# Projecting q and k of a head pair together, 512 moving columns at a time

## The chip, the cores and the metric

The kernel runs on one core of a Trainium2 chip. The metric is the device time of one execution in microseconds (us). The kernel before took 879.91, 881.80 and 883.73 us in three runs, median 881.8 us. Beside these, one execution was profiled; every duration below comes from it.

## The reference

One layer of a hybrid decoder on 512 tokens of width 1024, in float32:

```
h = rmsnorm(x)
[q | k | v | x_rnn | g_rnn | gate_attn | gate_rnn] = h @ W_in
A = differential attention (q and k normed per head half of 64, T5 bias, causal, 8 heads)
R = gelu(g_rnn) * RG-LRU(conv4(x_rnn))
x = x + (sigmoid(gate_attn) * (A @ P_attn) + sigmoid(gate_rnn) * (R @ P_rnn)) @ W_out
x = x + relu(rmsnorm(x) @ W_up)^2 @ W_down
```

q, k and v are 1024 wide each. A head has 128 columns of q and of k (two halves of 64, each with its own softmax; the second is subtracted with a learnt weight) and 128 of v.

## The kernel before, in words

**Numbers as pairs.** Every operand of a large matmul is a pair `hi`, `lo` in a rounded 32-bit format: ACT writes `hi` (a cast), DVE writes `lo` (source minus `hi`). A product is three matmuls, hi·hi, hi·lo, lo·hi (`mm3`, L124 to L127). The normed input is held as `hT`, transposed, in eight pieces of 128 features (k = 0 to 7).

**Weights.** `Weights` (L81) is a queue of units of 128 x 1024 numbers. SP fetches a unit into one of two raw buffers (`fetch`), ACT and DVE split it into a `whi`, `wlo` pair (`cast`). There are four pairs (`slots`); `get` takes the next unit, `free` gives its pair back, `pump` casts one more if a pair is free and fewer than `ahead` units are waiting.

**Stages.** An opening stage loads x, norms it and projects three gate blocks; then come attention, the recurrent branch, the merge and the MLP. The change lies in the end of the opening and in attention.

**A head pair.** `qkv_pair(j)` (L432) projects q, k and v of heads 2j and 2j+1. For each of the three, two units hold 4 k each of 256 weight columns. For each of four token tiles (128 tokens) `tok_proj` (L220) holds the tokens' piece of hT still in the array and moves the 256 weight columns past it: 8 k times 3 products, 24 matmuls with 256 moving columns. Two token tiles share a PSUM bank (`acc`, three banks). When a bank of q or k is full, `normed_a` squares it on ACT, sums the squares on DVE and takes the power -0.5 on POOL (`rs`); `normed_b` multiplies bank by `rs` into `qn` on DVE; `turn` transposes it on PE and splits it into `qkT`. A bank of v is split at once.

**The steps of attention.** 32 steps, four query tiles for each of eight heads. `logits(s)`: 6 small PE matmuls. `soft_a(s)`: DVE adds the bias and takes the maximum (two passes and `nm`), ACT takes the exponentials. `soft_b(s)`: four DVE operations that normalise and subtract. `turn(s)`: PE transposes the result, ACT and DVE split it into `pt`. `av`: PE multiplies by v. Step s issues logits(s), soft_a(s), soft_b(s-1) and turn(s-2):

```
order = [post_d, post_c, post_b, av, post_a, turn, logits, soft_a, soft_b]
```

Between steps `fill_in` runs pieces of the next pair's projection, by a budget of 3.6 a step; a token tile counts 2.6. Pair 0 is projected before the first step, pairs 1 to 3 during the 24 steps of pairs 0 to 2.

**What sets the order.** ACT, DVE and POOL keep the order in which the program issues (`InOrder`, L58), and each works strictly down its list in the profile. PE's list is set when the program is built: a scheduler takes, by its own estimate of times, what is ready first. On the chip PE works down that fixed list.

**Bias.** `toep`, eight resident tiles of 128 x 512, one per head, are loaded by SP from a table laid out in DRAM, in the first pair and the first steps.

Of the kernel before, what the change touches and what calls it, by code (L numbers as in the profile page):

```python
# [23 lines left out]
KT = DM // P  # L24
NH = 8
# [4 lines left out]
TW = 640  # L30
# [4 lines left out]


@with_exitstack
def tile_block(ctx: ExitStack, tc: tile.TileContext, x, w_in, w_rga, w_rgx, w_pa, w_pr, w_o,
               w_up, w_dn, rel_bias, smalls, lamv, onehot, out):
    nc = tc.nc  # L40

# [34 lines left out]
    def psum(tag):  # L76
        return pp.tile([P, 512], F32, tag=tag, name=tag, bufs=nb[tag])

    slots = [4]

    class Weights:  # L81
        def __init__(self, ahead, raws):
            self.reqs, self.raw, self.units = [], [], []
# [14 lines left out]
        def cast(self, pool=None):  # L98
            assert pool or slots[0] > 0
            slots[0] -= 0 if pool else 1  # L100
            self.fetch()
            n = len(self.units)
            raw, a = self.raw[n], self.reqs[n][1]
            hi, lo = ((pool or wp).tile([P, a, 1024 // a], F32R, tag=t, name=t, bufs=2 if pool else 4) for t in ("whi", "wlo"))
# [14 lines left out]
            return self.units[self.pos - 1]  # L119

        def free(self):
            slots[0] += 1

    def mm3(o, l, r, first, last):  # L124
        T.matmul(o, l[0], r[0], start=first, stop=False)  # L125
        T.matmul(o, l[0], r[1], start=False, stop=False)  # L126
        T.matmul(o, l[1], r[0], start=False, stop=last)  # L127
# [88 lines left out]
    def h_tok(k, t):  # L216
        ts = slice(t * P, (t + 1) * P)
        return hT[0][:, k, ts], hT[1][:, k, ts]

    def tok_proj(bank, ws, t):  # L220
        b = bank[:, 256 * (t % 2):256 * (t % 2) + 256]
        for k in range(KT):
            w = ws[k // 4]
            mm3(b, h_tok(k, t), (w[0][:, k % 4, :], w[1][:, k % 4, :]), k == 0, k == KT - 1)
            if t == NT - 1 and k % 4 == 3:
                wa.free()
        wa.pump()

    OQ, OK_, OV, OX, OG, OGA, OGR = (j * DM for j in range(7))
# [136 lines left out]
    def bias_table():  # L366
        parts = ((0, 512), (512, 128))
        ohs = []
        for c0, n in parts:
            o = work("oh")  # L370
            nc.sync.dma_start(o[:64, :n], onehot[:, c0:c0 + n])
            ohs.append(o)
        rb = sm.tile([64, 32], F32, name="rbt", tag="rbt", bufs=1)
        G.memset(rb, 0.0)
        G.memset(rb[32:33, :], MASKED)
        nc.sync.dma_start(rb[0:NBUCKET, 0:NH], rel_bias)
        yield
        for (c0, n), o in zip(parts, ohs):
            ps = psum("at")
            T.matmul(ps[:32, :n], rb, o[:64, :n], start=True, stop=True)  # L380
            tb = work("tb")
            V.tensor_copy(tb[:32, :n], ps[:32, :n])
            nc.sync.dma_start(tdram[:, c0:c0 + n], tb[:NH, :n])
        yield
        for h in range(NH):
            nc.sync.dma_start(trep[h].rearrange("o (r y) -> o r y", r=P),
                              tdram[h:h + 1, :].rearrange("h (o y) -> h o y", o=1).broadcast_to([1, P, TW]))
            yield
            t0 = trep[h][0:1, :]
            nc.sync.dma_start(toep[h], bass.AP(tensor=t0.tensor, offset=t0.offset + 127, ap=[[TW - 1, P], [1, S]]))  # L390

    def lam_diff(lt):
        lv = lt[:, :256].rearrange("p (a b c) -> p a b c", a=2, b=2)
# [36 lines left out]
        yield  # L430

    def qkv_pair(j, qk, v):  # L432
        def proj(o, bank):
            ws = [wa.get(), wa.get()]
            for t in range(NT):
                if t % 2 == 0:
                    bank.append(psum("acc"))
                tok_proj(bank[t // 2], ws, t)
                yield 2.6

        def normed_a(b, qn):
            n = wk.tile([P, S], F32, tag="qn", name="qn", bufs=4)
            A.activation(n, b, AF.Square)
            ss = sm.tile([P, 8], F32, tag="ss8", name="ss8")
            V.tensor_reduce(out=ss, in_=n.rearrange("p (g d) -> p g d", g=8), axis=AX.X, op=ALU.add)
            rs = sm.tile([P, 8], F32, tag="rs8", name="rs8")
            rstd_of(rs, ss, 64, 8)
            qn.append(n)
            return b, n, rs

        def normed_b(b, n, rs):
            V.tensor_tensor(out=n.rearrange("p (g d) -> p g d", g=8), in0=b.rearrange("p (g d) -> p g d", g=8),
                            in1=rs.rearrange("p (g o) -> p g o", o=1).broadcast_to([P, 8, 64]), op=ALU.mult)

        def turn(qi, qn, gsc, hh):
            ps = psum("at")
            for t in range(NT):
                c0 = 256 * (t % 2) + P * hh
                T.transpose(out=ps[:, t * P:(t + 1) * P], in_=qn[t // 2][:, c0:c0 + P], identity=ident)  # L459
            d = unit("qkT")  # L460
            split(d[:, 0, :], d[:, 1, :], ps, gsc)
            qk[hh, qi] = d

        banks = {o: [] for o in (OQ, OK_, OV)}
        qn = {o: [] for o in (OQ, OK_)}
        pend, half = [], []
        for o, qi, gsc in ((OQ, 0, qg), (OK_, 1, kg), (OV, None, None)):
            for t, cost in enumerate(proj(o, banks[o])):
                half.append(None)
                ready = half.pop(0) if len(half) > 2 else None  # L470
                if ready:
                    normed_b(*ready)
                if t % 2 == 1:
                    b = banks[o][t // 2]
                    if o != OV:
                        half[-1] = normed_a(b, qn[o])
                    else:
                        vt = wk.tile([P, 2, 2, 256], F32R, tag="v", name="v", bufs=4)
                        split(vt[:, 0], vt[:, 1], b.rearrange("p (t c) -> p t c", t=2))
                        v.append(vt)  # L480
                if pend and t >= 2:
                    turn(*pend.pop(0))
                    cost += 0.45
                yield cost
                if j == 0 and o == OV and t == 0:
                    lam_diff(lt)
                if j == 0 and o != OQ:
                    next(bt)
            if o != OV:
                pend = [(qi, qn[o], gsc, 0), (qi, qn[o], gsc, 1)]  # L490

    def attention(fills, qks, vs, pads):
        st = {}
# [97 lines left out]
        def at(step, f, *a):  # L591
            acts.setdefault(step, []).append((f, a))

        for s in range(NH * NT):
# [7 lines left out]
            if i == 3:  # L602
# [1 line left out]
                at(s + 4, post_b, h)  # L604
                at(s + 5, post_c, h)
                at(s + 7, post_d, h)
        order = [post_d, post_c, post_b, av, post_a, turn, logits, soft_a, soft_b]
        for step in sorted(acts):
            j = step // (2 * NT)
            if step >= 37:  # L610
                wb.pump()
            if step == 30:
# [12 lines left out]
            if step < NT * NH + 6:  # L625
                fill_in(fills[min(j + 1, NH // 2)], pads[min(j, NH // 2)])
# [514 lines left out]
```

## Time and profile before

| | |
|---|---|
| runs | 879.91, 881.80, 883.73 us; median 881.8 |
| profiled execution | 880.92 us, its span (first to last instruction) 879.2 us |
| busy of the span | PE 99%, weight loads (PEld) 87%, DVE 68%, ACT 49%, POOL 7% |
| granted TensorE clock | 1.00 |
| pair 0 projected | from 41.9 us to 79.7 us |
| first logits | 79.9 us |
| last logits (step 31) | 274.1 us |

In a row of the timeline the first number is the start in us from the span's beginning, the second the duration, then engine, line, operation and tiles (written <- read); "x6" means that six rows are merged. In a group's row the numbers after the count are the busy time in us and the mean ns of one. Matmuls overlap, so the start of one is not the end of the one before it. L66 is the helper through which all ACT, DVE and POOL operations go; there the tiles' names tell what is done. Pieces of 512 columns on one engine that follow each other directly start a little closer than their durations say.

### The profile page before, as it was taken

What the parts mean: (1) busy time and instruction counts of PE and PEld (TensorE: products, weight loads), DVE (VectorE), ACT (ScalarE), POOL (GpSimd) and SP (SyncE); (2) the same over time, 40 slices, a digit from 0 to 9 for tenths busy, and PEclk for the clock granted to TensorE, in tenths of its full rate; (3) what the DMA queues carried; (4) which work ended last, traced back from release to release, by engine and by line L of the source; (5) the groups of instructions that cost most, each with busy time, mean ns of one, the idle gap of its engine ahead of it and who ended that gap; (6) DMA issues with size and microseconds to landing.
All of it is one profiled execution on the core that took longest, in us unless ns stands there. A gap on an engine that the chain in (4) does not pass through costs nothing.

```text
span 879.2 us, 13193 instructions
## 1 busy us (share of the span) xinstructions
PE 871.2 (99%) x5232; PEld 762.6 (87%) x5232; DVE 602.2 (68%) x1040; ACT 429.0 (49%) x683; POOL 64.4 (7%) x72
## 2 busy tenths in 40 slices
PE   9999999999999999999999999999999999999997
PEld 7799999999888887888878888889988998899897
DVE  6765688887866346877876656767746775667586
ACT  7444355554555336577643235556335444544441
POOL 0030222113000000000000000000000000000000
PEclk9999999999999999999999999999999999999999
DMA  5347222131321342322213633223642364256353
GB/s 200 135 142 222 93 73 77 52 94 62 98 70 39 113 137 95 110 85 88 80 55 125 223 125 114 102 86 82 170 166 72 110 173 134 64 137 194 78 146 95
DMA packets 34238, 99.28 MB, mean 113 GB/s; under 512 B 3952, under 2 KB 8760, under 8 KB 34176
## 3 DMA queue, kind: packets, MB, share of 16 engines
q1 hardware_dynamic: 30976, 87.93, 30.3%
q0 software_dynamic: 3200, 10.50, 6.3%
q8 instruction: 41, 0.67, 0.3%
q14 instruction: 21, 0.17, 0.1%
HBM read 87.89 MB, written 4.76 MB: 105 GB/s over the span
## 4 chain that ended last, share of the span: by engine, by line
PE 88%; ACT 4%; DMA 3%; DVE 3%; issue 1%; SPq 0%; POOL 0%; ACTq 0%; DVEq 0%; POOLq 0%
PE acc L125 21%; PE acc L126 21%; PE acc L127 20%; PE acc L1093 17%; PE at L507 3%; DMA wraw<-in_w_in_dram 2%; ACT whi L66 1%; DVE wlo L66 1%; PE at L541 1%; PE at L126 1%; PE at L127 1%; PE at L125 1%; PE at L459 1%; PE at L572 1%; DMA xT<-in_x_dram 1%
## 5 line engine op out<-in xcount | busy, mean ns | idle before, releaser
L1093 PE MATMUL acc<-us,whi 128*128 128x256 f32 x896 | 158.9, 281 | 0.5 <-DVE x L66 0.5
L66 DVE TENSOR_TENSOR wlo<-wraw,whi 128x1024 fp32r<-128x1024 f32 (+2 forms) x86 | 96.9, 1148 | 67.9 <-ACT whi L66 67.6
L66 ACT CAST whi<-raw 128x1024 fp32r<-128x1024 f32 x88 | 90.5, 1048 | 104.2 <-DVE raw L66 39.4
L1093 PEld LDWEIGHTS acc<-us,whi 128*128 128x128 f32 x896 | 137.7, 189 | 1.2 <-DVE x L66 0.7
L1093 PE MATMUL acc<-us,wlo 128*128 128x256 f32 x448 | 125.4, 280 | 0.0
L66 DVE TENSOR_TENSOR wlo<-raw,whi 128x1024 fp32r<-128x1024 f32 x88 | 106.8, 1220 | 17.1 <-ACT whi L66 17.0
L125 PE MATMUL acc<-whi,hT 128*128 128x256 f32 x384 | 111.4, 290 | 0.0
L127 PE MATMUL acc<-whi,hT 128*128 128x256 f32 x384 | 108.9, 284 | 0.0
L126 PE MATMUL acc<-wlo,hT 128*128 128x256 f32 x384 | 108.9, 284 | 0.0
L66 ACT CAST whi<-wraw 128x1024 fp32r<-128x1024 f32 (+2 forms) x86 | 82.5, 982 | 50.0 <-DMA wraw<-in_w_in_dram 33.6
L126 PE MATMUL acc<-h2T,whi 128*128 128x512 f32 x256 | 100.5, 392 | 0.0
L125 PE MATMUL acc<-h2T,whi 128*128 128x512 f32 x256 | 100.1, 391 | 0.0
L127 PE MATMUL acc<-h2T,wlo 128*128 128x512 f32 x256 | 100.0, 390 | 0.0
L1093 PEld LDWEIGHTS acc<-us,wlo 128*128 128x128 f32 x448 | 84.2, 188 | 0.0
L125 PE MATMUL acc<-hT,whi 128*128 128x512 f32 x208 | 82.2, 395 | 0.0
L127 PE MATMUL acc<-hT,wlo 128*128 128x512 f32 x208 | 81.5, 392 | 0.0
L126 PE MATMUL acc<-hT,whi 128*128 128x512 f32 x208 | 81.5, 392 | 0.0
L125 PEld LDWEIGHTS acc<-whi,hT 128*128 128x128 f32 x384 | 73.2, 191 | 4.3 <-issue 3.0
L127 PEld LDWEIGHTS acc<-whi,hT 128*128 128x128 f32 x384 | 73.2, 191 | 0.8 <-issue 0.4
L126 PEld LDWEIGHTS acc<-wlo,hT 128*128 128x128 f32 x384 | 73.3, 191 | 0.7 <-issue 0.5
L66 ACT ACTIVATE pe<-pe,nm 128x128 f32<-128x128 f32 (+3 forms) x64 | 35.5, 556 | 65.4 <-DVE nm L66 65.4
L66 DVE TENSOR_TENSOR x<-acc,x 128x512 f32<-128x512 f32 x48 | 33.0, 688 | 40.9 <-PE acc L1093 31.5
(194 smaller groups left out, 1609.9 us busy)
## 6 DMA issues: line engine op xcount, KB each, us to landing
wraw<-in_w_in_dram SPq DMA_DIRECT2D x52, 512.0 KB, 3.5
raw<-in_w_up_dram SPq DMA_DIRECT2D x32, 512.0 KB, 4.4
raw<-in_w_dn_dram SPq DMA_DIRECT2D x32, 512.0 KB, 3.4
raw<-raw POOLq DMA_DIRECT2D x16, 512.0 KB, 4.5
wraw<-in_w_pa_dram SPq DMA_DIRECT2D x8, 512.0 KB, 4.3
wraw<-in_w_pr_dram SPq DMA_DIRECT2D x8, 512.0 KB, 3.4
wraw<-in_w_o_dram SPq DMA_DIRECT2D x8, 512.0 KB, 4.4
trep<-tdram SPq DMA_DIRECT2D x8, 320.0 KB, 4.9
```

Source lines behind the costliest of these rows:

```text
L66: ins = f(*a, **k)
L125: T.matmul(o, l[0], r[0], start=first, stop=False)
L126: T.matmul(o, l[0], r[1], start=False, stop=False)
L127: T.matmul(o, l[1], r[0], start=False, stop=last)
L459: T.transpose(out=ps[:, t * P:(t + 1) * P], in_=qn[t // 2][:, c0:c0 + P], identity=ident)
L507: T.matmul(lg[c][:, :N], qT[r, x0, i * P:(i + 1) * P], kT[r, y0, :N], start=a == 0, stop=a == 2)
L541: T.transpose(out=tp[:, b * P:(b + 1) * P], in_=st[s][:, b * P:(b + 1) * P], identity=ident)
L572: T.matmul(ps[:, t:t + 1], sq[:, t * P:(t + 1) * P], ones, start=True, stop=True)
L1093: T.matmul(b[:, 256 * u:256 * u + 256], l[:, i, P * u:P * u + P], act[:, r, f, i % 2], start=p in ("M1", "M2", "M5") and k == z == u == e ...
```

## The change

- **q and k together.** A new weight tensor `w_qk` holds, for each pair, 256 columns of q beside 256 of k. A unit is 2 k of 512 columns. `tok_proj` makes two passes (`half`) over the pair's four units, two token tiles (z = 0, 1) in each; a matmul moves 512 columns past the tokens and each token tile fills one bank. v is projected by the same code with 256 columns and two tiles to a bank. The four units of q and k are held from the first pass through the second, where each is freed when its second tile is done.
- **Norm.** `normed_a` now copies the bank to `qn` on ACT, squares the bank in place and sums from there; `normed_b` works in `qn` alone. A bank of q and k is thus free after the sum, not after `normed_b`. There are still four `normed_a`, four `normed_b` and four `turn` for a pair, the turns now all in the second pass of v.
- **Slots.** From the start of attention's pools to step 26 there is a fifth `whi`, `wlo` pair; `ahead` is 4 in place of 2 until step 22.
- **Bias.** Four bias tiles in place of eight; those of heads 4 to 7 are loaded into them at steps 5, 9, 13 and 17 (`place_bias`).

```diff
-    slots = [4]
+    slots, spare_pool, more = [4], [], [False]
...
+        def wide(self, w):
+            self.reqs += [(w[u], 2) for u in range(4)]
+            return self
...
+            self.own.append(spare_pool.pop() if spare_pool else None)
+            hi, lo = ((self.own[-1] or wp).tile([P, a, 1024 // a], F32R, tag=t, name=t, bufs=1 if self.own[-1] else 4) for t in ("whi", "wlo"))
...
-    wa = Weights(2, 2)
+    wa = Weights(4, 2)
     wa.cols(w_in, OGA + 512)
     for j in range(4):
-        for o in (OQ, OK_, OV):
-            wa.cols(w_in, o + 256 * j)
+        wa.wide(w_qk[j]).cols(w_in, OV + 256 * j)
...
-    toep = [wk.tile([P, S], F32, tag=f"toep{h}", name=f"toep{h}") for h in range(NH)]
+    toep = [None] * NH
+    slots[0] += 1
+    spare_pool.append(wk)
+    more[0] = True
...
+    def place_bias(h):
+        t0 = trep[h][0:1, :]
+        toep[h] = wk.tile([P, S], F32, tag="toep", name="toep", bufs=4)
+        nc.sync.dma_start(toep[h], bass.AP(tensor=t0.tensor, offset=t0.offset + 127, ap=[[TW - 1, P], [1, S]]))
...
+        def tok_proj(nu, width):
+            k_of = KT // nu
+            us = []
+            for half in range(2):
+                out = [psum("acc") for _ in range(width // 256)]
+                for u in range(nu):
+                    if half == 0:
+                        us.append(wa.get())
+                    hi, lo = us[u]
+                    for z in range(2):
+                        ts = slice((2 * half + z) * P, (2 * half + z) * P + P)
+                        o = out[z] if width == 512 else out[0][:, 256 * z:256 * z + 256]
+                        for k in range(k_of):
+                            kk = u * k_of + k
+                            for e, (l, r) in enumerate(((hT[0], hi), (hT[0], lo), (hT[1], hi))):
+                                T.matmul(o, l[:, kk, ts], r[:, k, :], start=kk == 0 and e == 0 and (z == 0 or width == 512),
+                                         stop=kk == KT - 1 and e == 2, skip_group_check=True)
+                        if z == 1 and half == 1:
+                            wa.free()
+                        wa.pump()
+                        yield out if u == nu - 1 and z == 1 else None

         def normed_a(b, qn):
             n = wk.tile([P, S], F32, tag="qn", name="qn", bufs=4)
-            A.activation(n, b, AF.Square)
+            A.copy(n, b)
+            A.activation(b, b, AF.Square)
             ss = sm.tile([P, 8], F32, tag="ss8", name="ss8")
-            V.tensor_reduce(out=ss, in_=n.rearrange("p (g d) -> p g d", g=8), axis=AX.X, op=ALU.add)
+            V.tensor_reduce(out=ss, in_=b.rearrange("p (g d) -> p g d", g=8), axis=AX.X, op=ALU.add)
...
+        for n, out in enumerate(tok_proj(4, 512)):
+            if out:
+                half = [normed_a(b, qn) for b in out]
+            if n in (10, 11):
+                normed_b(*half.pop(0))
+            yield 1.3
...
+        for n, out in enumerate(tok_proj(2, 256)):
+            cost = 1.3
+            if out:
+                vt = wk.tile([P, 2, 2, 256], F32R, tag="v", name="v", bufs=4)
+                split(vt[:, 0], vt[:, 1], out[0].rearrange("p (t c) -> p t c", t=2))
+                v.append(vt)
+            if n in (2, 3):
+                normed_b(*half.pop(0))
+            if n >= 4:
+                turn(*((0, qn, qg), (1, qn, kg))[n % 2], n // 2 - 2)
+                cost += 0.45
+            yield cost
...
+        for h in range(4, NH):
+            at(4 * h - 11, place_bias, h)
```

PE's list is made anew. Three places matter below. The first is on PE in the steps of pair 0, while pair 1 is projected: turn(0), logits(2), turn(1) (`at<-ident,pe` is a turn of attention, `at<-qkT` are logits, `acc<-` is projection). Before:

```order
L541 MATMUL at<-ident,pe 128x128 [waits DVE_49,PE_49]
L507 MATMUL at<-qkT 128x384 x4
L126 MATMUL acc<-wlo,hT 128x256
...
L127 MATMUL acc<-whi,hT 128x256
L541 MATMUL at<-ident,pe 128x128 [waits DVE_49]
L541 MATMUL at<-ident,pe 128x128
L507 MATMUL at<-qkT 128x512
```

Now:

```order
L561 MATMUL at<-ident,pe 128x128 [waits DVE_49,PE_49]
L527 MATMUL at<-qkT 128x384 x4
L561 MATMUL at<-ident,pe 128x128 [waits DVE_49]
L561 MATMUL at<-ident,pe 128x128
L527 MATMUL at<-qkT 128x512
L527 MATMUL at<-qkT 128x512 x4
L455 MATMUL acc<-whi,hT 128x512 [waits DVE_49]
```

The 20 matmuls of projection that stood between logits(2) and turn(1) are gone from there; behind logits(3) the first matmul of the second pass's second bank stands with a wait for DVE.

The second place is DVE at the end of pair 0's projection: the last `normed_b` ahead of the turns. Before, from the sum for the last bank of k on:

```order
L66 TENSOR_REDUCE ss_755<-qn 128x8 [waits Activation_49]
L66 TENSOR_SCALAR ms<-ss_755 128x8 [waits DVE_49]
L66 SCALAR_TENSOR_TENSOR qkT<-at,qg,qkT 128x512 [waits Activation_49]
L66 TENSOR_TENSOR wlo<-wraw,whi 128x1024 [waits DMAHW4_49,Activation_49]
L66 TENSOR_TENSOR lt<-lt 128x128 [waits DMAHW1_49]
L66 TENSOR_REDUCE ls<-lt 128x2 [waits DVE_49]
L66 SCALAR_TENSOR_TENSOR lneg<-le 128x1 [waits Activation_49]
L66 TENSOR_TENSOR wlo<-wraw,whi 128x1024 [waits DMAHW7_49,Activation_49]
L66 TENSOR_TENSOR qn<-acc,rs_757 128x512 [waits Pool_49]
L66 TENSOR_TENSOR v<-acc,v 128x512 [waits Activation_49]
```

Now, from the sum for the second pass's second bank on (`lt`, `ls`, `lneg` are the learnt weight of the second softmax):

```order
L66 TENSOR_REDUCE ss_659<-acc 128x8 [waits Activation_49]
L66 TENSOR_SCALAR ms<-ss_659 128x8 [waits DVE_49]
L66 TENSOR_TENSOR wlo<-wraw,whi 128x1024 [waits DMAHW0_49,PE_49,Activation_49]
L66 TENSOR_TENSOR lt<-lt 128x128 [waits DMAHW3_49]
L66 TENSOR_REDUCE ls<-lt 128x2 [waits DVE_49]
L66 SCALAR_TENSOR_TENSOR lneg<-le 128x1 [waits Activation_49]
L66 TENSOR_TENSOR qn<-qn,rs_652 128x512 [waits Pool_49]
L66 TENSOR_TENSOR v<-acc,v 128x512 [waits Activation_49]
L66 TENSOR_TENSOR qn<-qn,rs_661 128x512 [waits Pool_49]
```

Two `normed_b` now stand here with a split of v between them; on PE the 33 matmuls of v (24 of its first pass and 9 of the second) stand between the end of the bank and the transposes that need the first of them.

The third place is PE from turn(3) to turn(4), with `at<-pt` the products with v. Before:

```order
L541 MATMUL at<-ident,pe 128x128 x3
L507 MATMUL at<-qkT 128x256 x4
L459 MATMUL at<-ident,qn 128x128 [waits DVE_49]
L125 MATMUL at<-pt_471,v 128x256 [waits Activation_49]
L125 MATMUL acc<-whi,hT 128x256
L126 MATMUL at<-pt_472,v 128x256 [waits DVE_49]
...
L126 MATMUL acc<-wlo,hT 128x256
L127 MATMUL acc<-whi,hT 128x256
L541 MATMUL at<-ident,pe 128x128 [waits DVE_49,PE_49]
```

Now:

```order
L561 MATMUL at<-ident,pe 128x128 x3
L527 MATMUL at<-qkT 128x256 x4
L134 MATMUL at<-pt_475,v 128x256 [waits Activation_49]
L135 MATMUL at<-pt_476,v 128x256 [waits DVE_49]
L136 MATMUL at<-pt_475,v 128x256
...
L136 MATMUL at<-pt_475,v 128x256
L561 MATMUL at<-ident,pe 128x128 [waits DVE_49,PE_49]
```

Four transposes of `qn` and six matmuls of projection stood in between and are gone from there.

More of the change, by code (lines that the diff above doesn't have):

```diff
@@ L96, in fetch, with cast @@
                 self.raw.append(raw)
-        def cast(self, pool=None):
-            assert pool or slots[0] > 0
-            slots[0] -= 0 if pool else 1
+        def cast(self):
+            assert slots[0] > 0
+            slots[0] -= 1
             self.fetch()
@@ L121, in free @@
         def free(self):
-            slots[0] += 1
+            own = self.own[self.done]
+            self.done += 1
+            if own and more[0]:
+                spare_pool.append(own)
+            slots[0] += 0 if own and not more[0] else 1
     def mm3(o, l, r, first, last):
@@ L218, in h_tok @@
         return hT[0][:, k, ts], hT[1][:, k, ts]
[L220 to L229, printed above, removed]
-    wa = Weights(2, 2)
+    OV, OX, OG, OGA, OGR = (j * DM for j in range(5))
+    wa = Weights(4, 2)
     wa.cols(w_in, OGA + 512)
     for j in range(4):
-        for o in (OQ, OK_, OV):
-            wa.cols(w_in, o + 256 * j)
+        wa.wide(w_qk[j]).cols(w_in, OV + 256 * j)
     wa.cols(w_in, OGA + 768)
@@ L462, in turn @@
             qk[hh, qi] = d
[L464 to L490, printed above, removed]
+        qn, half, pend = [], [], []
+        for n, out in enumerate(tok_proj(4, 512)):
[4 more added lines that the diff above has]
+            yield 1.3
+            if j == 0 and n >= 8 and n % 2 == 1:
+                next(bt)
+        for n, out in enumerate(tok_proj(2, 256)):
[10 more added lines that the diff above has]
+            yield cost
+            if j == 0 and n == 1:
+                lam_diff(lt)
+            if j == 0 and n % 2 == 1:
+                next(bt)
     def attention(fills, qks, vs, pads):
@@ L606, in attention @@
                 at(s + 7, post_d, h)
-        order = [post_d, post_c, post_b, av, post_a, turn, logits, soft_a, soft_b]
+        for h in range(4, NH):
+            at(4 * h - 11, place_bias, h)
+        order = [place_bias, post_d, post_c, post_b, av, post_a, turn, logits, soft_a, soft_b]
         for step in sorted(acts):
@@ L611, in attention @@
                 wb.pump()
+            if step == 22:
+                wa.ahead = 2
+            if step == 26:
+                more[0] = False
+                if spare_pool:
+                    spare_pool.pop()
+                    slots[0] -= 1
             if step == 30:
```

29 lines of the change are left out of this document (11 added, 18 removed).

## The prediction

> **What bounds the kernel now.** I read the page first, by engine and by slices, then the rows of the projection's matmuls.
>
> ```profile
> PE 871.2 (99%) x5232; PEld 762.6 (87%) x5232; DVE 602.2 (68%) x1040; ACT 429.0 (49%) x683; POOL 64.4 (7%) x72
> PE   9999999999999999999999999999999999999997
> L125 PE MATMUL acc<-whi,hT 128*128 128x256 f32 x384 | 111.4, 290 | 0.0
> L125 PE MATMUL acc<-hT,whi 128*128 128x512 f32 x208 | 82.2, 395 | 0.0
> ```
>
> PE is busy 99% in every stage: a microsecond that PE saves, or waits, anywhere is one of the whole. The two groups seem to price the change at once: 290 ns for 256 columns, 395 ns for 512, so two old ones cost 185 ns more than one new one. That is the trap of this page: the durations overlap, and only the distance from start to start counts. The timeline of PE, then the windows over two unbroken stretches of the tile `acc` (start to last start, busy, and the count of matmuls):
>
> ```profile
> 67.58 0.28 PE L126 MATMUL acc<-wlo,hT 128*128 128x256 f32 x1
> 67.70 0.28 PE L127 MATMUL acc<-whi,hT 128*128 128x256 f32 x1
> 67.82 0.28 PE L125 MATMUL acc<-whi,hT 128*128 128x256 f32 x1
> ...
> 67.38:75.97 8.59, 8.59 (x72) 8.59 (x72) 1.28 (x2) 1.03 (x2) 1.00 0.73 214
> ...
> 32.31:41.70 9.39, 9.39 (x42) 7.70 (x41) 0.00 (x0) 0.00 (x0) 1.00 0.29 109
> ```
>
> With 256 columns a matmul starts every 8.59/71 = 0.1210 us, with 512 every 9.39/41 = 0.2290 us. The engines beside PE in the steps of attention (PE, PEld, DVE, ACT, POOL busy in each 20 us):
>
> ```profile
> 100.00:120.00 20.00, 20.00 (x165) 18.45 (x165) 17.33 (x54) 10.42 (x26) 5.94 (x3) 1.00 0.17 54
> 120.00:140.00 20.00, 20.00 (x164) 18.59 (x163) 17.36 (x48) 11.74 (x27) 4.01 (x4) 1.00 0.35 111
> ```
>
> DVE works 87% of the time there, in a fixed order. It keeps up because PE always finds projection to do meanwhile.
>
> **What PE saves.** q and k took 768 matmuls of 256 columns (two thirds of 3 x 384); they become 384 of 512. Each saves 2 x 0.1210 - 0.2290 = 0.013 us; 384 x 0.013 = **5.0 us**. By neighbouring stretches both distances move by some 2 ns: bounds 3 and 6.5 us. Turns, logits and v keep their matmuls.
>
> [...]
>
> **What is added beside PE.** Sixteen copies of a bank on ACT, about 0.58 us each as the square in the first row of the next fence: 9.3 us over 170 us on an engine that is about half busy; it costs only where PE waits for the norm, priced below. `normed_b` reads `qn` in place of a bank: the same 512 columns, taken as nothing. The four later bias loads wait on SP for a tile whose last reader stands two steps earlier, and have eleven steps to land: nothing; were that cover gone, the weight fetches behind them would be late too, a landing each. The fifth slot holds the first unit of v while the other four hold q and k: no cost of its own.
>
> **Where PE now waits.** Four places, read from the new lists and priced by rows of before.
>
> *Turn(1) behind logits(2).* ACT, DVE and PE at that place before:
>
> ```profile
> 99.70 0.58 ACT L66 ACTIVATE qn<-acc 128x512 f32<-128x512 f32 x1
> ...
> 98.28 0.17 DVE L66 TENSOR_SCALAR nm<-mx 128x2 f32<-128x2 f32 x1
> 98.36 0.16 DVE L66 RECIPROCAL rc<-sums 128x2 f32<-128x2 f32 x1
> 99.06 0.48 DVE L66 SCALAR_TENSOR_TENSOR pe<-pe,r 128x256 f32<-128x256 f32 x1
> 100.31 0.69 DVE L66 TENSOR_REDUCE ss<-qn 128x8 f32<-128x512 f32 x1
> ...
> 96.38 0.79 PE L507 MATMUL at<-qkT 64*128 64x384 f32 x6
> 97.10 0.39 PE L126 MATMUL acc<-wlo,hT 128*128 128x256 f32 x1
> 99.60 0.44 PE L541 MATMUL at<-ident,pe 128*128 128x128 f32 x2
> 99.97 0.96 PE L507 MATMUL at<-qkT 64*128 64x512 f32 x6
> 100.86 0.38 PE L125 MATMUL acc<-whi,hT 128*128 128x256 f32 x1
> ```
>
> soft_b(1) stands behind soft_a(2) on DVE, and that needs logits(2). So logits(2) from 96.38 lead to the end of soft_b(1) at 99.06 + 0.48 = 99.54, and turn(1) at 99.60. Before, 20 matmuls of projection filled 97.10 to 99.60. Now they are gone: **2.5 us** of waiting (2.0 to 2.9). Then logits(3) run to 100.86, and the next matmul needs the bank of the first pass back. ACT is done with the exponentials at 99.70; copy and square take about 0.5 each at their real spacing, the sum on DVE 0.69, with 0.2 for the handovers: 101.6. That is **0.8 us** more (0 to 1.5).
>
> *Turn(4) behind turn(3).*
>
> ```profile
> 112.15 0.60 PE L541 MATMUL at<-ident,pe 128*128 128x128 f32 x4
> 113.23 0.66 PE L459 MATMUL at<-ident,qn 128*128 128x128 f32 x4
> 113.64 0.36 PE L125 MATMUL at<-pt,v 128*128 128x256 f32 x1
> 113.84 0.29 PE L125 MATMUL acc<-whi,hT 128*128 128x256 f32 x1
> 114.15 0.38 PE L126 MATMUL at<-pt,v 128*128 128x256 f32 x1
> 115.56 0.28 PE L127 MATMUL acc<-whi,hT 128*128 128x256 f32 x1
> 116.03 0.30 PE L541 MATMUL at<-ident,pe 128*128 128x128 f32 x1
> ...
> 115.53 0.35 DVE L66 SCALAR_TENSOR_TENSOR pe<-pe,r 128x128 f32<-128x128 f32 x1
> ```
>
> From turn(3), the split of `pt`, soft_a(5) and soft_b(4) end at 115.53 + 0.35 - 112.15 = 3.7 us. PE took 3.88 us for the way. Without the transposes of `qn` (113.23 to 113.64) and the projection (113.84 to 114.15, 115.56 to 116.03) it takes 2.7: **1.0 us** (0.5 to 1.5).
>
> *Pair 0, the second bank.* PE's new list runs 18 matmuls into the first bank, then needs a bank that a gate product on DVE still reads; one more cast now stands ahead of it.
>
> ```profile
> 40.16 1.22 DVE L66 TENSOR_TENSOR wlo<-wraw,whi 128x1024 fp32r<-128x1024 f32 x1
> 44.71 1.28 DVE L66 TENSOR_TENSOR gate<-acc,rb 128x512 f32<-128x512 f32 x2
> ...
> 41.93 0.28 PE L125 MATMUL acc<-whi,hT 128*128 128x256 f32 x1
> ```
>
> The first of the two gate products ends near 45.4, with the cast 46.6; PE arrives at 41.93 + 18 x 0.229 = 46.05: **0.6 us** (0 to 1.5).
>
> *Pair 0, the turns of q and k.*
>
> ```profile
> 70.51 0.29 DVE L66 TENSOR_TENSOR lt<-lt 128x128 f32<-128x128 f32 x1
> 71.39 0.16 DVE L66 SCALAR_TENSOR_TENSOR lneg<-le 128x1 f32<-128x1 f32 x1 [0.27 <-ACT le L66]
> 73.47 0.69 DVE L66 TENSOR_TENSOR qn<-acc,rs 128x512 f32<-128x512 f32 x1
> 74.07 0.68 DVE L66 TENSOR_TENSOR v<-acc,v 128x512 fp32r<-128x512 f32 x1
> ```
>
> Count from the end of the second pass. Copy and square end at 1.1, the cast on ACT behind them at 2.1, its part on DVE (1.2, as above) at 3.35, `lt` to `lneg` (1.0) at 4.35; then `normed_b`, v and `normed_b` at 0.6 each: 4.95, 5.55, 6.15. PE has 33 matmuls of v, 4.0 us, and two transposes, 4.25: it waits 0.7 for the third, does four small matmuls and waits again, 0.75. **1.5 us** (0.7 to 2.5; more if the cast's raw tile lands late).
>
> *The rest of pairs 1 to 3.* In the new list the turns there stand at least as far apart as the 3.7 us that the loop above needs, and PE has projection between logits and turns; the margins are a few tenths. I take **0.5 us** (0 to 4).
>
> **Sum.** 0.6 + 1.5 + 2.5 + 0.8 + 1.0 + 0.5 = 6.9 us of waits against 5.0 saved: +1.9. From the profiled execution's 880.9 that is 882.8, say **883 us**. The profiled execution lies 0.9 below the median of the runs (881.8), within their spread. Less than 0.5%, 4.4 us, cannot be told from no change here: the forecast is no change.
>
> **Rivals.** *Slower: DVE falls behind in pairs 2 and 3 too.* For: 87% busy, margins of tenths, and PE's list was fitted to estimated times. Against: before, the same order of steps ran without a wait. If the projections of pairs 2 and 3 each repeat the first place's loss (3.3 us with the bank), the waits grow by 6.6 - 0.5 = 6.1: 889 us. It decides once DVE or ACT is some 0.5 us later per step than the rows say. Chance 0.27.
>
> *Faster: the waits are smaller.* Only turn(1) is sure; if the list leaves 2.5 us and the saving is 6.5: 877 us. For: some waits overlap, since PE's pause lets DVE catch up. Against: the four places lie 10 us or more apart. Chance 0.13.
>
> *The matmul is bounded by loading the held tokens, and 512 columns run at the durations' price.* For: the groups' means; PEld busy in 8.59 of 8.59 us at 256 columns, in 7.70 of 9.39 at 512. Then 384 x (2 x 0.290 - 0.395) = 71 us go: 810 us. Against: the start distances, 0.229 in a stretch where PEld had room. Chance 0.02. [...]
>
> **How the numbers follow.** The forecast has 0.58, the rivals 0.27, 0.13 and 0.02. Faster 0.15, same 0.58, slower 0.27. The forecast's own range is its terms' bounds taken half way, 879.5 to 886; for 8 in 10 it reaches to the faster rival's edge and most of the way into the slower: 878 to 890.
>
> **What would show it.** In the new profile: `acc<-whi,hT` with 512 columns, starts 0.229 apart; PE idle or stretched for 2 to 3 us between logits(2) and turn(1) near 97 us, with DVE `pe` as releaser; a shorter gap behind logits(3), released by DVE `ss`; gaps near 46, 70 and 110 us. Later stages unchanged but shifted. I am wrong if starts at 512 columns stand nearer than 0.22, if PE shows no gap at the first place, or if gaps recur with every pair.

## The result and the profile after

The changed kernel takes **889.2 us** (median of 5 runs, 887.04 to 889.76) against 880.9 (5 runs beside it, 879.91 to 883.73): the ratio of the means is 1.0085, 95% interval 1.0064 to 1.0107. It is slower by 0.85%, some 7.5 us, and that is clear of noise. The forecast was no change, at 883.0, and anything under 0.5% was to count as that; the range 878 to 890 holds the time by 0.8 us. The profiled execution is the fastest of the five, 887.04 us with a span of 885.2.

The page, by engine and by slices (before: 871.2 us at 99%, and a row of nines):

```profile
PE 871.2 (98%) x4848; PEld 742.1 (84%) x4848; DVE 602.7 (68%) x1040; ACT 436.8 (49%) x699; POOL 62.1 (7%) x72
PE   9999899999999999999999999999999999999997
L455 PE MATMUL acc<-whi,hT 128*128 128x512 f32 (+1 forms) x512 | 133.1, 342 | 1.2 <-DVE ss L66 0.8
```

384 matmuls are gone from PE (5232 to 4848), and one slice has an 8. The view of waits, for PE from 40 to 320 us, was empty before. Now (waiting engine, tile and line, what released it: us in total, times, longest):

```profile
PE at L561 <- DVE pe L66: 2.4, 1, 2.4
PE acc L455 <- DVE ss L66: 0.8, 1, 0.8
PE at L592 <- ACT osq L66: 0.7, 2, 0.4
PE at L134 <- ACT pt L66: 0.7, 1, 0.7
PE acc L455 <- DVE gate L66: 0.4, 1, 0.4
PE at L135 <- DVE pt L66: 0.3, 1, 0.3
PE at L561 <- DVE tmp L66: 0.3, 1, 0.3
```

The first row is turn(1) behind logits(2), as forecast, in PE's timeline:

```profile
96.44 0.79 PE L527 MATMUL at<-qkT 64*128 64x384 f32 x6
99.67 0.69 PE L561 MATMUL at<-ident,pe 128*128 128x128 f32 x2 [2.44 <-DVE pe L66]
100.28 1.65 PE L527 MATMUL at<-qkT 64*128 64x512 f32 x6
101.86 0.79 PE L455 MATMUL acc<-whi,hT 128*128 128x512 f32 x1
102.45 0.63 PE L455 MATMUL acc<-wlo,hT 128*128 128x512 f32 x1
```

The row of logits(3) holds the surprise: 1.65 us for six matmuls that took 0.96 before. Windows of 1 us there (PE, PEld, DVE, ACT, POOL busy; then the granted clock of PE):

```profile
97.00:98.00 1.00, 0.23 (x4) 0.00 (x0) 0.87 (x4) 0.00 (x0) 0.00 (x0) 1.00 0.00 0
...
99.00:100.00 1.00, 0.34 (x2) 0.29 (x2) 0.69 (x3) 1.00 (x5) 0.00 (x0) 0.84 0.00 0
100.00:101.00 1.00, 1.00 (x6) 0.62 (x6) 0.16 (x1) 1.00 (x3) 0.00 (x0) 0.50 0.00 0
101.00:102.00 1.00, 1.00 (x7) 0.35 (x3) 0.86 (x3) 1.00 (x3) 0.12 (x1) 0.50 0.00 0
102.00:103.00 1.00, 1.00 (x3) 0.81 (x4) 0.97 (x4) 0.11 (x1) 1.00 (x1) 0.50 0.00 0
103.00:104.00 1.00, 1.00 (x6) 0.83 (x5) 1.00 (x4) 0.00 (x0) 1.00 (x2) 0.95 0.00 0
```

After the pause PE gets **half its clock** for 2 x (0.16 + 0.50 + 0.50 + 0.50 + 0.05) = 3.4 us. Before, the clock was 1.00 from 10 to 870 us. The five runs after have mean clocks of 0.998, 0.995, 0.997, 0.995 and 0.998.

**Where the time went.** From the first projection matmul to the first `xh,gw` matmul of the recurrent stage, all distances between PE's starts summed by kind (worked out from all matmul records of the profiled executions; "projection" are the matmuls that read `hT`; a distance counts with the matmul at its start, so a wait counts with the matmul ahead of it):

```
                     start   projection  other  sum     after it  span
before               41.93   224.74      73.50  298.24  538.99    879.15
changed              41.04   224.03      81.41  305.44  538.76    885.24
width undone         41.35   227.75      80.12  307.88  538.69    887.92
gap filled           41.93   225.51      77.96  303.47  538.68    884.09
first four steps     43.11   223.59      77.94  301.52  538.75    883.39
three pairs          42.27   222.86      78.49  301.35  538.91    882.52
before, three pairs  41.88   223.66      78.82  302.47  538.94    883.29
three pairs, narrow  41.85   225.72      79.96  305.68  539.00    886.53
```

All of it is lost in attention: +7.2 us there, -0.2 after it (the start varies from 41.0 to 43.1 from kernel to kernel, with nothing changed ahead of it). The column of projection shrinks by only 224.74 - 224.03 = 0.7 us, since waits and slow clock that fall on projection are in it too. The other rows are the experiments below.

### The profile page after: what moved, and what is told of

Its sections match the earlier page's. It is cut to its first block, busy times and chain, and to the rows that moved or that the text cites. A ratio compares the mean times of both kernels' runs of the same rounds, so it can differ in the third digit from the quotient of the medians.

```text
span 885.2 us, 12445 instructions
## 1 busy us (share of the span) xinstructions
PE 871.2 (98%) x4848; PEld 742.1 (84%) x4848; DVE 602.7 (68%) x1040; ACT 436.8 (49%) x699; POOL 62.1 (7%) x72
## 4 chain that ended last, share of the span: by engine, by line
PE 85%; ACT 5%; DVE 5%; DMA 2%; issue 1%; SPq 0%; POOL 0%; ACTq 0%; DVEq 0%; POOLq 0%
PE acc L1122 17%; PE acc L134 16%; PE acc L135 16%; PE acc L136 16%; PE acc L455 13%; PE at L527 2%; DVE wlo L66 1%; ACT whi L66 1%; PE at L561 1%; PE at L134 1%; PE at L481 1%; PE at L136 1%; PE at L135 1%; DVE pe L66 1%; PE at L592 1%
## 5 line engine op out<-in xcount | busy, mean ns | idle before, releaser
L455 PE MATMUL acc<-whi,hT 128*128 128x512 f32 (+1 forms) x512 | 133.1, 342 | 1.2 <-DVE ss L66 0.8
L455 PEld LDWEIGHTS acc<-whi,hT 128*128 128x128 f32 x512 | 88.7, 190 | 13.8 <-issue 1.2
L455 PE MATMUL acc<-wlo,hT 128*128 128x512 f32 (+1 forms) x256 | 87.5, 342 | 0.0
L134 PEld LDWEIGHTS acc<-h2T,whi 128*128 128x128 f32 x256 | 48.1, 188 | 10.7
L136 PEld LDWEIGHTS acc<-h2T,wlo 128*128 128x128 f32 x256 | 48.1, 188 | 10.4
L135 PEld LDWEIGHTS acc<-h2T,whi 128*128 128x128 f32 x256 | 48.1, 188 | 10.1
```

Source lines behind the costliest of these rows:

```text
L455: T.matmul(o, l[:, kk, ts], r[:, k, :], start=kk == 0 and e == 0 and (z == 0 or width == 512), stop=kk == KT - 1 and e == 2, skip_group_ch ...
```

## The experiments

They ask three things: what the parts of the change are worth, what the pause at 97 us costs, and whether an order of PE's matmuls exists that keeps the saving. Every time is a median; each ratio is one of means, against runs of the kernel before on the same chip. A difference of two such ratios is uncertain by some 1.5 to 2.5 us.

**The order of PE's list.** PE's list in the changed kernel is built from estimated times. The first runs hold the program's order instead:

```diff
-                if self.engine in last:
+                if self.engine in last and (self.engine is not nc.tensor or pin[0]):
...
-    V, A, G, T = InOrder(nc.vector), InOrder(nc.scalar), InOrder(nc.gpsimd), nc.tensor
+    pin = [False]
+    V, A, G, T = InOrder(nc.vector), InOrder(nc.scalar), InOrder(nc.gpsimd), InOrder(nc.tensor)
...
+            pin[0] = 0 <= step < 40
```

In the second run the last line has 8 in place of 40.

> The changed kernel with one difference: during attention the matmuls stand on PE in the order in which the program writes them (two tiles of projection between steps), instead of the list that was fitted to estimated times. Theory 1, the built list: the 10 us of gaps arise where logits(0) and (1) stand behind half of pair 1's projection and turns and logits then follow each other bare. In program order 2.9 to 4.1 us of projection stand between the steps, so the 2.77 us gap near 97, the clock below 1.00 behind it and the bank's 1.1 us near 120 go; the narrower saving of some 4 us is left: 876 to 880 us, mean clock 1.000, no gap over 1 us. Theory 2, the work beside PE (copies, in-order DVE and ACT, the bank held through the norm) sets the pace whatever the list: 886 to 891 us, the gaps come back at other places.

> As before it, but the program's order holds on PE only in the first eight steps of attention (pair 0 and the first pass of pair 1); from step 8 the list is built as in the changed kernel. Theory 1 in the form that the first place is the cause: nearly all of the gain of the full order, 878 to 882 us. If the later gaps (near 166, 176, 277 us; 2.3 us together) matter, the two kernels differ by 1.5 to 3 us. Theory 2: 886 to 891 us.

The same lines in the kernel before:

> The control: the kernel before, with PE in program order during attention, as in the first run. Theory 1: its list left no waits over 0.4 us, so nothing is to be gained: 879 to 883 us, or slower by 1 to 3 us where narrow fillers of 2.9 us between the steps don't cover DVE. If it gains 3 us or more, the order is worth something by itself, and the first run's gain is not the change's.

Measured: 894.2 us (1.0143, 1.0129 to 1.0157), 886.0 (1.0050, 1.0037 to 1.0062) and 889.4 (1.0095, 1.0080 to 1.0109). The first theory in this form falls: held through all of attention, the program's order is worse for both kernels. The control lost some 8 us, more than anything expected of it. PE's waits in the first run:

```profile
PE at L66 <- DVE pe L66: 5.3, 4, 1.7
PE acc L66 <- DVE gate L66: 3.1, 1, 3.1
```

The program alternates pair 0's two banks from the start and so meets the gate product's bank 3.1 us too early; the built list runs 18 matmuls into the first bank and waits 0.4. And turn(3) of pairs 0 to 2 has too little projection ahead of it and waits up to 1.7 us each time, in the kernel before too (pauses of 1.5 us, three times). Some 4 us of the first and third runs lie behind attention (543.5 and 543.0 us against 539.0), where an order held to step 39 reaches into the next stage. The second run shares the costly start, and is still 3 us faster than the changed kernel: what its first eight steps leave out, the place at 97 us with them, is worth more than that.

**The slots.** The changed kernel with four slots and eight bias tiles:

```diff
-    toep = [None] * NH
-    slots[0] += 1
-    spare_pool.append(wk)
-    more[0] = True
+    toep = [wk.tile([P, S], F32, tag=f"toep{h}", name=f"toep{h}") for h in range(NH)]
...
```

> The changed kernel without its second part: four weight slots in attention and eight resident bias tiles, as before. Theory 1: this part has no hand in the loss; 887 to 891 us, unless the first unit of v, cast one unit later, makes PE wait at the end of each projection (then 1 to 3 us more). Rival 3, the fifth slot's earlier cast on ACT and DVE and the bias loads make the work beside PE late: 880 to 884 us.

888.5 us, 1.0080 (1.0067 to 1.0092), against 1.0085: no difference that can be told. Leaving out the fifth slot and the four bias tiles does not bring the loss back, as the prediction took them; a cost of a microsecond or two is not excluded, since the list built without them has its waits at other places: no long pause at 97 us, but 1.9 us for a bank near 117.

**The width alone, in the built list.**

```diff
-                                T.matmul(o, l[:, kk, ts], r[:, k, :], start=kk == 0 and e == 0 and (z == 0 or width == 512),
-                                         stop=kk == KT - 1 and e == 2, skip_group_check=True)
+                                for y in range(width // 256):
+                                    T.matmul(o[:, 256 * y:256 * y + 256], l[:, kk, ts], r[:, k, 256 * y:256 * y + 256],
+                                             start=kk == 0 and e == 0 and y == 0 and (z == 0 or width == 512),
+                                             stop=kk == KT - 1 and e == 2, skip_group_check=True)
```

> The changed kernel with its stages, copies, slots and two passes, but each matmul of 512 columns split into two of 256: the width alone is undone. By the prediction's term (384 x 0.013 us) it is 5.0 us (3 to 6.5) slower than the changed kernel, about 894 us; by the changed kernel's own distances between its gaps (236 ns a matmul with all short stalls, against two of 123.6) 4.1 us, about 893 us. If the width saves nothing, it stays at 889. PE's list is built anew and can move a wait or two, some 2 us either way.

891.0 us, 1.0109 (1.0095 to 1.0123): 2.1 us slower than the changed kernel by the two ratios, whose intervals overlap. In the profiled executions the projection takes 227.75 - 224.03 = 3.7 us more, and the rest 1.3 less. That a part of what the width saves comes back as waits, since wider projection covers the chain beside it for less time, would fit this but is not shown: PE's idle time in the two views of waits is nearly the same, and the pause of 2.4 us with its half clock stands in both.

**The pause filled.** The same work, and 20 matmuls more that nobody reads:

```diff
...
             st[s] = lg
+            if s == 2:
+                ps = psum("at")
+                for n in range(20):
+                    d = T.matmul(ps[:, :256], hT[0][:, 0, :P], hT[0][:, 0, :256], start=True, stop=True)
+                    after(d, m)
+                    m = d
+                tail[0] = m
...
```

`after` sets the order on PE: the logits, these twenty, turn(1).

> The changed kernel with 20 matmuls of 256 columns more, whose result nobody reads, placed on PE between logits(2) and turn(1), where PE stood for 2.77 us: 2.4 us of work in a wait of 2.65. No work is taken away and the wait's end is set by DVE, so without an effect on the clock the time stays at 889. Clock theory: the half clock that follows the pause by some 3.4 us and lasts for 3 us (1.4 us lost in the profiled run, more in the runs with a mean clock of 0.995) goes with the pause: 885 to 888 us, mean clock 0.999 to 1.000.

**885.9 us** (885.57 to 886.42), 1.0051 (1.0039 to 1.0064): 3 us faster than the changed kernel with more work on PE, and the mean clock is 0.999 or 1.000 in all five runs. By the two traces PE's order is otherwise the same but for one matmul of projection, which stands 1 us later. PE's timeline, and two windows:

```profile
97.31 0.79 PE L531 MATMUL at<-qkT 64*128 64x384 f32 x6
98.03 2.64 PE L536 MATMUL at<-hT 128*128 128x256 f32 x20
100.53 0.44 PE L572 MATMUL at<-ident,pe 128*128 128x128 f32 x2
100.90 0.96 PE L531 MATMUL at<-qkT 64*128 64x512 f32 x6
102.46 0.50 PE L455 MATMUL acc<-whi,hT 128*128 128x512 f32 x1 [0.60 <-DVE ss L66]
```

```profile
101.00:102.00 1.00, 0.86 (x6) 0.39 (x6) 0.28 (x1) 1.00 (x3) 0.00 (x0) 1.00 0.00 0
102.00:103.00 1.00, 0.54 (x2) 0.48 (x3) 0.86 (x3) 0.98 (x3) 0.24 (x1) 1.00 0.00 0
```

Logits(3) are back at 0.96 us. And the bank that the prediction put behind them, missing above because the half clock stretched the logits over it, is now a wait of 0.60, released by DVE `ss`. So the clock behind the pause is a cost of its own: some 3 us over the runs, about as much as the pause, of which the profiled execution shows 1.7. (The expectation has the half clock 3.4 us behind the pause; by the changed kernel's trace it begins as the pause ends, at 99.68, 2.8 us after the pause's start at 96.90.)

**The bank freed by the square.**

```diff
+            sq = wk.tile([P, S], mybir.dt.bfloat16, tag="sqn", name="sqn")
             A.copy(n, b)
-            A.activation(b, b, AF.Square)
+            A.activation(sq, b, AF.Square)
...
-            V.tensor_reduce(out=ss, in_=b.rearrange("p (g d) -> p g d", g=8), axis=AX.X, op=ALU.add)
+            V.tensor_reduce(out=ss, in_=sq.rearrange("p (g d) -> p g d", g=8), axis=AX.X, op=ALU.add)
```

> The changed kernel with one difference in the norm: the square goes to a tile in SBUF (in bf16, so the norm is a little rougher) instead of back into the bank, so the bank is free when ACT has squared it and doesn't wait for the sum on DVE. If the bank's hold through the norm is a main cause, the waits of projection for a bank (1.0 us near 120, 0.55 near 45 is another bank) go and the list keeps more projection between the steps: 885 to 887.5 us. If the waits come from the chain of logits, DVE and turns, no change: 888 to 890 us.

886.6 us, 1.0060 (1.0046 to 1.0073), with runs from 885.73 to 889.65. The wait of PE for DVE `ss` is gone from the view of waits, a saving of 0.7 us between starts near 121. The rest of the difference cannot be put down to it: two of the five runs (885.73 and 886.42) had a mean clock of 1.000, three 0.997, and the profiled one, of the three, still has the 2.4 us pause.

**Orders meant to keep the saving.** The order of the first run, from step 0 to 31, with pair 0's projection left to the list and more projection ahead of turn(3):

```diff
                 run(fills[j])
                 owed[0] = 0.0
+            pin[0] = 0 <= step < 32
...
-                fill_in(fills[min(j + 1, NH // 2)], pads[min(j, NH // 2)])
+                fill_in(fills[min(j + 1, NH // 2)], pads[min(j, NH // 2)] + (1.6 if step % 8 == 4 else 0.0))
```

> The changed kernel with PE in program order from the first step of attention to step 31, but pair 0's projection left to the built list (its program order cost 3.3 us of waiting and a slow clock at 43 us in the first two runs), and with 1.6 us more of projection between logits(4) and turn(3) of each pair, where the first run waited 1.9 us three times. Theory, the change's saving of 4 to 5 us is real and all its losses are waits of the order: attention without gaps over 1 us, 875 to 879 us. Rival, DVE and ACT set the pace and a gap that is filled comes back elsewhere: 882 to 890 us.

(Of the first two runs only the second had a slow clock near 43 us, at 47.5.)

890.3 us, 1.0099 (1.0085 to 1.0113): the rival. Until logits(8) it was ahead, 85.6 us from the first projection matmul against 88.5 before and 95.1 in the changed kernel. Then PE waits in the projections of pairs 2 and 3:

```profile
PE at L66 <- DVE qn L66: 6.3, 5, 2.0
```

With more projection drawn early, the transposes of `qn` come a step sooner, and the second product with the norm, on DVE behind the softmax, has not run. Both pauses are followed by half a clock for 6.8 us (0.992 in the mean).

The order in the first four steps alone (`pin[0] = 0 <= step < 4`, pads as they were):

> The changed kernel with PE in program order in the first four steps of attention alone (without pair 0's projection): logits(0) come ahead of pair 1's projection as before, near 79 us instead of 86.8. Late-start theory: the changed kernel loses because PE does 7 us of projection while DVE has no steps to do (0.77 of 10 us busy from 80 to 90), and lacks it later as cover; with the early start logits(8) come near 128 (before 130.5, changed 136.2), the 2.77 us gap and the low clock go, and the time is 878 to 882 us. Rival, the waits come back in the list behind step 4 whatever the start: 885 to 889 us.

883.9 us, 1.0037 (1.0026 to 1.0049): 4.2 us faster than the changed kernel by the ratios, the 2.4 us wait gone, the mean clock 0.999 or 1.000. That is the first place's price, pause and clock, measured by its removal; added up from the pause (2.65) and the filled pause's gain (3) it would be 5.7, which the uncertainty allows. But the late-start theory falls: logits(8) come at 134.3, not near 128, since the built list behind step 4 keeps its other waits nearly as they were:

```profile
PE acc L66 <- DVE ss L66: 0.8, 1, 0.8
PE at L66 <- ACT osq L66: 0.7, 2, 0.4
PE at L66 <- ACT pt L66: 0.5, 1, 0.5
PE acc L66 <- DVE gate L66: 0.4, 1, 0.4
```

The last three hold one order and compare what the width is worth in it (`pin[0] = 0 <= step < 24`, and 1.6 us of pad moved from step 5 to step 4 of each eight): the changed kernel, the kernel before, and the changed kernel with its matmuls split as above.

> The changed kernel with PE in program order from the first step to step 23, pair 0's projection and all after step 23 left to the list, and 1.6 us of projection moved from behind turn(3) of each pair to ahead of it (the first run waited 1.9 us there, and turn(4) had 4.5 us to spare). Theory, the saving of 4 us is real and the losses are all waits of the order: no gap over 1 us in attention, mean clock 0.999 to 1.000, 875 to 879 us, faster than the kernel before. Rival, a filled gap comes back elsewhere, as in the last run at the transposes of qn: 883 to 890 us.

> The control: the kernel before with the same order on PE and the same shift of projection around turn(3). If the order is worth something by itself, it gains too: below 880 us. If its list was already full, 880 to 884 us; and where its granules of 2.9 us leave turn(3) or turn(4) uncovered, up to 888. The width with its stages is then worth the difference to the run before this one: 4 to 6 us by theory.

> The kernel of the ordered run of three pairs (884.29 us), with each matmul of 512 columns split into two of 256 and every other instruction of PE in the same order: the width alone, with the list held still. If what the width saves on PE reaches the end, it is slower by the pitch, 384 x (2 x 0.1236 - 0.2350) = 4.7 us: about 889 us. If the engines beside PE take the saved time back as waits, as in the run that undid the width in the built list (+1.7 us instead of 4.5), it is slower by 1 to 2.5 us: 885.3 to 887, with shorter gaps near 111, 169 and 223 us and a mean clock nearer to 1.000.

884.3 us (1.0034, 1.0022 to 1.0046), 885.0 (1.0044, 1.0031 to 1.0057) and 888.4 (1.0081, 1.0066 to 1.0095). No kernel here beats the one before. In the first of them PE still waits at turn(5) of pairs 1 and 2:

```profile
PE at L66 <- DVE po L66: 1.6, 1, 1.6
PE at L66 <- DVE den L66: 1.6, 1, 1.6
PE at L66 <- DVE tmp L66: 0.9, 3, 0.3
```

The releasers named are the next small operations on DVE; the softmax's last product for that turn ends 0.16 us before it. Around the first of these waits DVE is full:

```profile
169.00:170.00 1.00, 0.36 (x4) 0.27 (x3) 0.93 (x7) 0.28 (x1) 0.00 (x0) 1.00 0.00 0
170.00:171.00 1.00, 0.07 (x1) 0.10 (x2) 0.96 (x4) 1.00 (x5) 0.00 (x0) 1.00 0.00 0
...
173.00:174.00 1.00, 1.00 (x7) 1.00 (x6) 1.00 (x4) 0.00 (x0) 0.97 (x1) 0.50 0.00 0
```

The width, with the order of PE's list held still, comes to 888.4 - 884.3 = **4.1 us** (uncertain by some 1.6), near the 4.7 of its expectation. The table of PE's starts has 225.72 - 222.86 = 2.9 of it in the projection (3.8 without its waits for a gate bank and for weights, which are longer in the wide kernel) and 1.5 in the rest, most of that clock: logits of 512 columns behind the waits at 171 and 227 us ran at half clock in the narrow kernel. In the wide one the same wait at 223 us brought no half clock, so part of the 4.1 is the clock's and not the width's; the one narrow run at a mean clock of 0.999 took 885.7.

## Why the prediction held in its range and failed in its sum

The step that failed is the sum of waits, in two terms above all: "the rest", set at 0.5 us and near 3.9 when measured, and a cost that the sum did not have, the clock behind the first pause. Term by term, from the profiled executions:

- **What PE saves**, 5.0 (bounds 3 to 6.5): 3.7 in the built list, 3.8 in the held one, both against the same kernel with its matmuls split. The mechanism held: in an unbroken stretch of the changed kernel 31 distances of 512 columns took 7.10 us, 0.229 each:

```profile
88.91:96.01 7.10, 7.10 (x32) 5.82 (x31) 0.00 (x0) 0.00 (x0) 1.00 0.25 76
```

  The size came out a quarter smaller: outside such stretches distances are longer (before, 0.1236 us on average over the 1152 matmuls of 256 columns, against 0.1210 in the stretch of the prediction), which the two undisturbed stretches did not show. The rival of 512 columns at the durations' price is out.
- **Turn(1) behind logits(2)**, 2.5: 2.44 idle. Right, place and releaser too.
- **The bank behind logits(3)**, 0.8: none in the changed kernel, 0.60 where the pause is filled. Right in kind; the half clock covered it.
- **Its clock**, not in the sum: 3.4 us at half, 1.7 of it lost, in the profiled execution; by the filled pause, 3 us over the runs. The prediction has no such term, and every cost was worked out at a clock of 1.00. With it the first place costs 4.2 us instead of 3.3, by the run that removed it.
- **Turn(4) behind turn(3)**, 1.0 (0.5 to 1.5): from turn(3) at 115.6 to turn(4) at 119.5 PE starts late three times, by 0.3, 0.6 and 0.45. 1.35 in all, within its bounds. The latter two, and the bank behind logits(6) that belongs to "the rest":

```profile
117.60 0.38 PE L135 MATMUL at<-pt,v 128*128 128x256 f32 x1 [0.34 <-DVE pt L66]
119.48 0.30 PE L561 MATMUL at<-ident,pe 128*128 128x128 f32 x1 [0.30 <-DVE tmp L66]
121.29 0.39 PE L455 MATMUL acc<-whi,hT 128*128 128x256 f32 x1 [0.79 <-DVE ss L66]
```

- **Pair 0, the second bank**, 0.6: 0.4 idle, 0.55 between starts, released by the gate product. Right.
- **Pair 0, the turns of q and k**, 1.5: nothing. The first product with the norm on DVE came as counted (it ends at 70.0, 4.9 us behind the pass, 4.95 forecast), but the cover was miscounted: not 33 matmuls of v stand ahead of the transposes but 60 (48 of v's first pass and 12 of its second), 7.1 us from 64.94 to 72.08.

```profile
69.31 0.69 DVE L66 TENSOR_TENSOR qn<-qn,rs 128x512 f32<-128x512 f32 x1
72.08 0.49 PE L481 MATMUL at<-ident,qn 128*128 128x128 f32 x3
```

- **The rest**, 0.5 (0 to 4): near 3.9. A bank again, behind logits(6) this time (0.79 idle, 1.0 between starts), and seven late starts in pairs 1 to 3, of the products with `pt`, of the sums of `osq` and of logits, by 0.2 to 0.8 each. Inside the bounds, at their far end. It was the term with the widest bounds, and was set near their lower end because the kernel before showed no wait; a list that is built anew carries no such promise.

Waits of 8.5 us (2.65 + 1.35 + 0.55 + 3.9 between starts) instead of 6.9 and 1.6 of slow clock, against 3.7 saved, make +6.4; the table's difference is +7.2, and the 0.8 between them is not traced to a place. Against the forecast's +1.9 the kernel lost 5.3 more: 3.4 in the rest, 1.6 in the clock, 1.3 in the smaller saving, 0.5 in turn(1) and turn(4) and the 0.8, less 2.3 for the two terms that came out at nothing. That those two made up for so much was luck: without their 2.3 us the time would have been near 891.5, outside the range. With a start 0.9 earlier and 0.2 less behind attention, +7.2 is the profiled execution's 887.0; the other runs, at mean clocks of 0.995 to 0.998, lie 2 to 3 us above it.

The slower rival named 889 us, but not for its reason. "DVE falls behind in pairs 2 and 3 too", with 3.3 us in each, did not happen: no wait there is longer than 0.9. The faster rival is out: the waits were larger.

Not settled: which order, if any, keeps the 4 us. In those held over more than four steps a wait that was taken away came back at another place, and with one order held for both kernels the change as a whole gains 884.3 - 885.0 = -0.7 us, within the intervals. What the four runs of the changed kernel 2 to 3 us above the profiled one lost, and where, no profile shows; their clocks alone do not order them (889.13 us at 0.998, 889.22 at 0.995).

## What to carry to other kernels

Price a pause of the bounding engine by what follows it, too: here 2.7 us without a matmul cost 1.6 us more in clock in the profiled execution and some 3 over the runs, and useless matmuls in the pause bought it back (889.2 to 885.9 us). Where PE's work is also the cover of a tight chain on another engine, a saving on PE can be paid back as waits (here 8.5 us of them against 3.7 saved), and a list built anew puts them at places that the old trace cannot show; for that term take the middle of its bounds, not the end at which the old kernel stood. Test a width with the order of the list held still, or the list's changes hide it.

## What the hardware showed

The half clock after a pause of PE, in all profiled executions with a pause of over 1.2 us in attention (distance of starts; stretch by windows of 1 us, length as twice the missing clock):

```
kernel                pause at, us          half clock from, for
changed               96.9, 2.77            99.7, 3.4
four slots            116.9, 2.25           120.0, 6.8
width undone          98.9, 2.77            101.9, 3.4
bank freed early      98.3, 2.77            101.7, 3.4
all in order          43.1, 3.50            none
                      106.9, 2.08           109.9, 3.4
                      160.7, 1.98           164.5, 3.4
                      214.6, 1.96           none
first eight steps     42.8, 3.51            47.5, 3.4
                      108.2, 2.08           none
before, all in order  1.53, three times     none
after pair 0          168.5, 2.27 and 1.36  171.5, 6.8
                      225.1, 2.26 and 1.35  229.5, 6.8
three pairs           169.1, 1.82           172.6, 3.4
                      223.4, 1.81           none
three pairs, narrow   171.6, 1.82           173.9, 3.4
                      226.8, 1.82           228.5, 3.4
```

The half clock followed three of the four pauses of 1.81 or 1.82 us, one of the two of 2.08, and that of 3.51 us but not that of 3.50. After the three of 1.53 us there was none. It begins 1.7 to 4.7 us after the pause's start, so it falls on the work behind it, and lasts 3.4 or 6.8 us. What decides which pauses it follows, and whether it lasts 3.4 or 6.8 us, these runs do not show.

The clock records of the changed kernel's trace have 95.57 us at 1.00 up to 99.68, then 3.413 at 0.50, then 781.65 at 1.00; those of the kernel before have 873.81 us at 1.00, from 5.9 us to past the end of its span. By the windows, two half clocks of one execution start 54.6 us apart with all in order (109.9 and 164.5) and in three pairs, narrow (173.9 and 228.5), and 58.0 after pair 0 (171.5 and 229.5). 95.57, 781.65 and 873.81 are close to 28, 229 and 256 times 3.413, and 54.6 and 58.0 to 16 and 17 times that.
